# A dense gated layer's first matrix by seven products of quarters in place of eight

## The chip, the cores and the metric

One core of one Trainium2 chip runs the whole program. The metric is device microseconds of one execution. Engines are named as the profile names them: PE (TensorE, with its weight loads as PEld), DVE (VectorE), ACT (ScalarE), POOL (GpSimd) and SP (the queue that issues most transfers).

## The reference, cut to what matters

Two decoder layers for 520 tokens (512 of a prompt and 8 samples), 1024 channels. The change touches the dense gated layer that ends layer 0, and the place of a small compression step of layer 1:

```python
def rmsnorm(x, g):
    x32 = x.astype(F32)
    y = x32 * lax.rsqrt(jnp.mean(x32 * x32, axis=-1, keepdims=True) + EPS) * g.astype(F32)
    return y.astype(x.dtype)

def swiglu(h, w_in, w_out):          # D_FF = 2816
    a, b = jnp.split(h @ w_in, 2, axis=-1)
    return (jax.nn.silu(a) * b) @ w_out
```

Layer 0 is: norm, state-space mixer with a gated output (GELU, then `a * sigmoid(b)`), residual add; norm, `swiglu`, residual add. Layer 1 compresses blocks of the cached rows with a small two-layer network (first matrix 2048 to 128, GELU, second matrix) before its attention.

## The kernel before, in words

Channels lie on the 128 partitions and tokens along a row, so the activations of 1024 channels are a tile of 128 x 8 x 520. Every product is made of f16 parts: an f32 value x is split into a high part xh (ACT copies it to f16) and a low part xl (DVE or POOL subtracts xh from x), and a product is wh·xh + wh·xl + wl·xh, three matmuls that add up in PSUM. `mm3` (from line 230) runs over k (128 input channels each), over the three pairs of parts, and over two column ranges, 256 and 264 tokens. Weights arrive as f32 (`wload`, from line 214): a transfer on the SP queue, an ACT instruction for the high part (line 222), a DVE instruction for the low part (line 223), for 2048 columns at a time; the f32 tile and both f16 tiles have two buffers.

The stages around the change, in order:

- The gated output of the mixer: eight blocks of 2 x 8 x 3 x 2 = 96 matmuls. After each block ACT and DVE empty PSUM (lines 297, 298) and POOL adds to the residual stream `XT` and squares it for the next norm (lines 299, 264, 265).
- `norm` (line 244): two ones-matmuls add up the squares over the partitions (line 249), ACT takes the root, DVE the reciprocal (line 251); then for each of the 8 channel groups k DVE scales (line 254), ACT makes the high part `GH` (line 255), and DVE and POOL in turn make the low part `GL` (line 257).
- `cache_compress`, a generator called with `next`: loads 16 pages of cached rows and splits them (lines 203, 205), loads and splits the first matrix, multiplies the position part (96 matmuls of one column, line 803), and then runs 192 matmuls of 120 columns for the first half of the rows (line 818), before it yields; the second half runs when it is called again after the dense layer. PE has it to do while `norm` is made.
- The dense layer's first matrix: 22 blocks `ob`, each with a transfer of 1 MB, one ACT and one DVE instruction to split it, 96 matmuls, then per column range one ACT Silu (line 324) and one DVE product with the other half (line 325), an ACT copy to f16 `UH` (line 327) and a POOL subtraction to `UL` (line 328).
- The second matrix: 8 blocks over 22 input groups, `XT` updated (line 337), the next norm.

The order of the instructions on each engine's queue is fixed when the program is built, by a planner that gives an earlier line of the source the first turn among what it takes to be ready. On the chip each engine takes its queue strictly in that order. PSUM has 8 banks, handed out in turn by `PS()`.

Of the kernel before, what the change touches and what calls it, by code (L numbers as in the profile page):

```python
# [18 lines left out]
NT = 520  # L19
WS = 256.0  # L20
# [144 lines left out]
def build(tc, a, o, stop=None):  # L165
    nc = tc.nc
    es = ExitStack()
    with es:
# [59 lines left out]
        HV = ((0, 256), (256, NT))  # L228

# [13 lines left out]
        def norm(act, acc, gain):  # L243

            rs = act_pool.tile([128, NT], F32, tag="rs", name=f"rs{cnt[0]}")
            for c0, c1 in HV:
# [4 lines left out]
                V.reciprocal(rs[:, c0:c1], rs[:, c0:c1])  # L251
            for k in range(8):
# [4 lines left out]
                e.tensor_tensor(GL[:, k, :], h, GH[:, k, :], op=ALU.subtract)  # L257

# [30 lines left out]


        for ob in range(8):
            wh, wl = glu_first[ob] if ob < 2 else glu_w(ob)
# [12 lines left out]
        norm(XT, acc, gains[:, 0, :])  # L305
        cs = {}
        cache = cache_compress(tc, nc, a, PS, csp, w1p, wload, hilo, cs)
        next(cache)
        with tc.tile_pool(name="ffn", bufs=1) as fp:

            z = fp.tile([128, 2048], F16, name="z")
# [4 lines left out]
            UH = fp.tile([128, 22, NT], F16, name="UH")  # L316
            UL = fp.tile([128, 22, NT], F16, name="UL")
            for ob in range(22):
                wh, wl = wload(a["w_fin"][:, 2 * ob:2 * ob + 2].rearrange("p b k c -> p (b k c)"), 2048, f"f{ob}")
# [8 lines left out]
                G.tensor_tensor(UL[:, ob, :], sg, UH[:, ob, :], op=ALU.subtract)  # L328
            for ob in range(8):
# [428 lines left out]
def cache_compress(tc, nc, a, PS, cs, w1p, wload, hilo, out):  # L758
# [14 lines left out]
    with tc.tile_pool(name="cc", bufs=1) as cp:  # L773
# [3 lines left out]
        nc.sync.dma_start(wc2, a["w_c2"].rearrange("e s f -> e (s f)"))  # L777
        CS = []
        for b2 in range(4):
            CSH = cp.tile([128, 2, 2, 4, 128], F16, name=f"CSH{b2}")  # L780
            CSL = cp.tile([128, 2, 2, 4, 128], F16, name=f"CSL{b2}")
# [29 lines left out]
        for s in range(2):  # L811
            if s:
                yield
# [1128 lines left out]
```

## Time and profile before

| | us |
|---|---|
| median of 3 runs | 1485.88 (1482.97 to 1486.5) |
| profiled execution, its own time | 1482.78 |
| its span in the trace | 1481.0 |
| first matrix of the dense layer, first to last matmul | 234.0 to 470.2 |

The span is what the trace covers of the profiled execution; its own time is 1.8 us longer for what lies around it. "Busy" of an engine is time in which an instruction of it runs. In a timeline a line is a run of equal instructions: start, the time from the first's start to the last's end, what it is, how many; a bracket gives the idle time ahead of it and what ended that. An instruction that has been issued and is held up inside its engine counts as running.

### The profile page before, as it was taken

Reading aid. Unit: us, or ns where it says so; the run is one execution under the profiler, and the core shown is the slowest. Engines: PE = TensorE matmul, PEld = TensorE weight load, DVE = VectorE, ACT = ScalarE, POOL = GpSimd, SP = SyncE. Lnnn points to the kernel's source line nnn. Section 1 sums busy time; section 2 is a strip of 40 time slices with the busy share of each in tenths; the row PEclk is TensorE's granted clock in tenths of the full one; section 3 lists DMA queues with packets and bytes.
Section 4 is the critical chain, followed back from the end, with each engine's and each line's share of the span. In section 5 each row is a group of like instructions: output and inputs, shape, how many; then the busy total and the mean of one; then the engine's idle time right before and its main releaser. Section 6 shows DMA issues by size and latency. Waiting matters only on the chain. (4 is left out here: it accounts for less than half of the span.)

```text
span 1481.0 us, 37495 instructions
## 1 busy us (share of the span) xinstructions
PE 1355.3 (92%) x15657; PEld 1177.6 (80%) x15657; DVE 943.0 (64%) x1643; ACT 767.4 (52%) x1418; POOL 543.9 (37%) x464
## 2 busy tenths in 40 slices
PE   3869999999999999989989989979997999999994
PEld 2848888888888888766776757848877999999993
DVE  9885565323232323594887886477756888878885
ACT  5526344223232112343887776456645767867772
POOL 4991442222221222211122233306811632724835
PEclk8879999999999999999999999989999999999997
DMA  4124752222322334253313211148999999999984
GB/s 169 61 70 159 263 184 76 96 104 91 110 89 76 120 116 153 93 161 116 100 58 116 82 49 51 46 185 290 357 263 306 369 306 387 361 307 370 325 306 143
DMA packets 82048, 262.34 MB, mean 177 GB/s; under 512 B 25242, under 2 KB 40082, under 8 KB 64338
## 3 DMA queue, kind: packets, MB, share of 16 engines
q1 hardware_dynamic: 78770, 249.24, 49.3%
q0 software_dynamic: 2816, 8.52, 1.7%
q8 instruction: 124, 2.03, 0.6%
q10 hardware_dynamic: 288, 2.14, 0.4%
q14 instruction: 50, 0.41, 0.1%
HBM read 232.30 MB, written 21.67 MB: 171 GB/s over the span
## 5 line engine op out<-in xcount | busy, mean ns | idle before, releaser
L1599 DVE SCALAR_TENSOR_TENSOR ml<-mf,mh 128x2048 f16<-128x2048 f32 (+1 forms) x152 | 310.5, 2046 | 77.1 <-ACT mh L1598 74.3
L1760 PEld LDWEIGHTS <-mh 128*128 128x128 f16 x4224 | 328.9, 98 | 17.9 <-ACT mh L1598 6.5
L1598 ACT ACTIVATE mh<-mf 128x2048 f16<-128x2048 f32 (+1 forms) x152 | 256.0, 1685 | 113.3 <-DMA mf<-in_w_mi 34.9
L1760 PE MATMUL ps<-XE,mh 128*128 128x64 f16 (+7 forms) x2816 | 280.3, 230 | 6.2 <-ACT mh L1598 4.6
L1760 PE MATMUL ps<-XE,ml 128*128 128x96 f16 (+7 forms) x1408 | 262.9, 230 | 2.4 <-DVE ml L1599 2.3
L1840 POOL TENSOR_TENSOR AL<-u,AH 128x272 f16<-128x272 f32 (+3 forms) x88 | 170.0, 1935 | 207.0 <-ACT AH L1839 205.8
L1760 PEld LDWEIGHTS <-ml 128*128 128x128 f16 x2112 | 205.1, 98 | 11.1 <-DVE ml L1599 4.6
L238 PEld LDWEIGHTS <-whf 128*128 128x128 f16 x1408 | 137.7, 98 | 20.2 <-issue 1.7
L238 PE MATMUL ps<-GL,whf 128*128 128x256 f16 x704 | 135.7, 274 | 1.0 <-DVE GL L257 1.0
L238 PE MATMUL ps<-GH,whf 128*128 128x256 f16 x704 | 135.8, 274 | 0.0
L238 PE MATMUL ps<-GH,wlf 128*128 128x256 f16 x704 | 135.6, 274 | 0.0
L1760 PE MATMUL ps<-AH,mh 128*128 128x144 f16 (+7 forms) x704 | 132.1, 229 | 1.5 <-ACT mh L1598 1.5
L1760 PE MATMUL ps<-AL,mh 128*128 128x272 f16 (+7 forms) x704 | 132.6, 229 | 0.9 <-POOL AL L1840 0.9
L1760 PE MATMUL ps<-AH,ml 128*128 128x144 f16 (+7 forms) x704 | 132.1, 229 | 1.3 <-DVE ml L1599 1.3
L328 POOL TENSOR_TENSOR UL<-sf,UH 128x520 f16<-128x520 f32 x22 | 59.4, 2700 | 176.0 <-ACT UH L327 176.0
L325 DVE SCALAR_TENSOR_TENSOR sf<-ps,sf 128x256 f32<-128x256 f32 (+1 forms) x44 | 16.9, 424 | 141.1 <-PE ps L238 141.1
L222 ACT ACTIVATE whf<-wff 128x2048 f16<-128x2048 f32 x22 | 42.0, 1910 | 95.2 <-issue 77.2
L238 PEld LDWEIGHTS <-who 128*128 128x128 f16 x704 | 68.9, 98 | 9.3
L238 PEld LDWEIGHTS <-wlf 128*128 128x128 f16 x704 | 68.9, 98 | 9.2
L1301 ACT ACTIVATE st<-st,mx 128x512 f32<-128x512 f32 (+3 forms) x128 | 71.6, 560 | 6.9 <-DVE mx L1299 6.1
L1299 DVE CUSTOM_DVE_ANT_0 st<-ps,BB 128x512 f32<-128x512 f32 (+3 forms) x128 | 61.2, 485 | 17.7 <-PE ps L1309 15.5
L1309 PE MATMUL ps<-identf,st 128*128 128x128 f32 x320 | 59.9, 288 | 11.8 <-DVE tl L205 7.9
(554 smaller groups left out, 3231.9 us busy)
## 6 DMA issues: line engine op xcount, KB each, us to landing
mf<-in_w_mi SPq DMA_DIRECT2D x88, 1024.0 KB, 7.1
mf<-in_w_mo SPq DMA_DIRECT2D x64, 704.0 KB, 5.8
wff<-in_w_fin SPq DMA_DIRECT2D x22, 1024.0 KB, 4.8
wfo<-in_w_fout SPq DMA_DIRECT2D x16, 704.0 KB, 4.1
wfg<-in_w_glu SPq DMA_DIRECT2D x8, 1024.0 KB, 4.7
wfq<-in_w_qk SPq DMA_DIRECT2D x8, 1024.0 KB, 4.8
HS<-z SPq DMA_DIRECT2D x9, 512.0 KB, 6.0
st<-in_ckc SPq DMA_DIRECT2D x16, 256.0 KB, 3.2
```

Of the source, the lines that this page charges most:

```text
L222: S.activation(wh[:, c], wf[:, c], AF.Copy, scale=WS)
L238: T.matmul(t[:, :c1 - c0], w[:, k0 + k, :], x[k][:, c0:c1] if isinstance(x, list) else x[:, k, c0:c1], start=(first and k == 0 and wi == 0 ...
L325: V.scalar_tensor_tensor(sg[:, c0:c1], tb_[:, :c1 - c0], IWS, sg[:, c0:c1], op0=ALU.mult, op1=ALU.mult)
L328: G.tensor_tensor(UL[:, ob, :], sg, UH[:, ob, :], op=ALU.subtract)
L1299: V.tensor_tensor_reduce(out=st[:, :N], in0=pS[:, :N], in1=bias_cur[0][:, r, 512 - N:], scale=1.0, scalar=3.0e38, op0=ALU.add, op1=ALU.min ...
L1301: S.activation(st[:, :N], st[:, :N], AF.Exp, bias=mx, scale=-1.0, accum_out=st8["sums"][:, 1 + br, r:r + 1])
L1309: T.transpose(pT[:, kb * 128:(kb + 1) * 128], st[:, kb * 128:(kb + 1) * 128], identf)
L1598: S.activation(wh, wf, AF.Copy, scale=WS)
L1599: V.scalar_tensor_tensor(wl, wf, WS, wh, op0=ALU.mult, op1=ALU.subtract)
L1760: T.matmul(ps, w[:, k0 + k, :], x[:, k, :], start=(k == 0 and i == 0), stop=(k == kn - 1 and i == 2))
L1840: al = G.tensor_tensor(AL[r][:, ob], u, AH[r][:, ob], op=ALU.subtract)
```

## The change

The product of the 1024 x 5632 matrix with 1024 x 520 activations is cut into quarters and made by seven products for eight (the Strassen scheme in Winograd's form). Per block `ob`, the weights of a and b and the two halves of the input channels are the four quarters of the weights, each 512 x 128; the two halves of the channels and the two halves of the tokens (260 each) are the four quarters of the activations. `seven` takes the place of `norm`: it makes the four scaled quarters and four sums of them in f32, and splits all seven factors into f16 parts. For each block four sums of weight quarters are made in f32 (three by DVE, one by POOL), and seven factors, 3584 columns for 2048, are split. Each product has 4 x 3 = 12 matmuls of 260 columns. Three PSUM banks hold pairs of products (one holds three); DVE adds between them in five instructions a block. The seventh product of a block and its last steps (`finish`) are put behind the first product of the next block, and a POOL product of the two halves comes new. `cache_compress` is called for its loads, its splits and its position part ahead of block 4 of the mixer's gated output; its first 192 matmuls are called behind that stage and ahead of `seven`. Its split rows become two tiles for one, and the first half's memory is given back before the dense layer.

```diff
+        def seven(act, acc, gain, X, sums):
+            rs = inverse(acc)
+            for k in range(4):
+                h = sums[:, k % 2]
+                for i, q in ((k, h[:, 0:8:7]), (k + 4, h[:, 3:5])):
+                    V.scalar_tensor_tensor(q, act[:, i, :]..., gain[:, i:i + 1], rs..., op0=ALU.mult, op1=ALU.mult)
+                V.tensor_tensor(h[:, 1], h[:, 7], h[:, 0], op=ALU.subtract)
+                G.tensor_tensor(h[:, 5], h[:, 4], h[:, 7], op=ALU.subtract)
+                V.tensor_tensor(h[:, 2], h[:, 4], h[:, 1], op=ALU.subtract)
+                V.tensor_tensor(h[:, 6], h[:, 3], h[:, 2], op=ALU.subtract)
+                for i, c in enumerate((slice(0, 4), slice(4, 7))):
+                    S.copy(X[0][i][:, :, k], h[:, c])
+                    (V, G)[i].tensor_tensor(X[1][i][:, :, k], h[:, c], X[0][i][:, :, k], op=ALU.subtract)
...
         for ob in range(8):
+            if ob == 4:
+                next(cache)
...
-        norm(XT, acc, gains[:, 0, :])
-        cs = {}
-        cache = cache_compress(tc, nc, a, PS, csp, w1p, wload, hilo, cs)
         next(cache)
...
+            sums = fp.tile([128, 2, 8, TH], F32, tag="UL", name="sums")
+            seven(XT, acc, gains[:, 0, :], XS7, sums)
...
-            for ob in range(22):
-                wh, wl = wload(a["w_fin"][:, 2 * ob:2 * ob + 2]..., 2048, f"f{ob}")
-                pa = mm3(wh, wl, 0, 8, GH, GL)
-                pb = mm3(wh, wl, 8, 8, GH, GL)
-                sg = act_pool.tile([128, NT], F32, tag="t2", name=f"sf{ob}", bufs=4)
-                for (c0, c1), ta, tb_ in zip(HV, pa, pb):
-                    S.activation(sg[:, c0:c1], ta[:, :c1 - c0], AF.Silu, scale=IWS)
-                    V.scalar_tensor_tensor(sg[:, c0:c1], tb_[:, :c1 - c0], IWS, sg[:, c0:c1],
-                                           op0=ALU.mult, op1=ALU.mult)
+            def finish(ob, w, b, q, uu, sg):
+                prod(b, w, xs(6), False)
+                V.scalar_tensor_tensor(uu[:, :TH], b[:, :TH], IWS, q[:, :TH], op0=ALU.mult, op1=ALU.add)
+                G.tensor_tensor(sg, sg, uu, op=ALU.mult)
                 S.copy(UH[:, ob, :], sg)
                 G.tensor_tensor(UL[:, ob, :], sg, UH[:, ob, :], op=ALU.subtract)
+            left = None
+            for ob in range(22):
+                wf = wst.tile([128, 4, 512], F32, tag="wf", name=f"wf{ob}")
+                nc.sync.dma_start(wf, a["w_fin"]...)
+                sw = fp.tile([128, 4, 512], F32, tag="sw", name=f"sw{ob}")
+                V.tensor_tensor(sw[:, 0], wf[:, 2], wf[:, 3], op=ALU.add)
+                G.tensor_tensor(sw[:, 2], wf[:, 0], wf[:, 2], op=ALU.subtract)
+                V.tensor_tensor(sw[:, 1], sw[:, 0], wf[:, 0], op=ALU.subtract)
+                V.tensor_tensor(sw[:, 3], wf[:, 1], sw[:, 1], op=ALU.subtract)
+                wa = [wst.tile([128, 4, 512], F16, tag=f"w{x}", name=f"w{x}f{ob}") for x in "hl"]
+                wb = [fp.tile([128, 3, 512], F16, tag=f"w{x}s", name=f"w{x}s{ob}", bufs=2) for x in "hl"]
+                for d, src in ((0, wf[:, 0]), (slice(0, 3), sw[:, 1:4]), (3, sw[:, 0]), (1, wf[:, 1]), (2, wf[:, 3])):
+                    h, l = (wb if src is sw or isinstance(d, slice) else wa)
+                    S.activation(h[:, d], src, AF.Copy, scale=WS)
+                    V.scalar_tensor_tensor(l[:, d], src, WS, h[:, d], op0=ALU.mult, op1=ALU.subtract)
+                prod(pa, wq(wa, 0), xs(0), True)
+                S.activation(q[:, :TH], pa[:, :TH], AF.Copy, scale=IWS)
+                if left is not None:
+                    finish(*left)
+                prod(pb, wq(wb, 0), xs(2), True)
+                V.scalar_tensor_tensor(q[:, TH:], pb[:, :TH], IWS, q[:, :TH], op0=ALU.mult, op1=ALU.add)
+                prod(pc, wq(wa, 3), xs(1), True)
+                V.scalar_tensor_tensor(uu[:, TH:], pc[:, :TH], IWS, q[:, :TH], op0=ALU.mult, op1=ALU.add)
+                prod(pa, wq(wa, 1), xs(3), False)
+                S.activation(sg[:, :TH], pa[:, :TH], AF.Silu, scale=IWS)
+                prod(pb, wq(wb, 1), xs(5), False)
+                V.scalar_tensor_tensor(uu[:, TH:], pb[:, :TH], IWS, uu[:, TH:], op0=ALU.mult, op1=ALU.add)
+                prod(pc, wq(wb, 2), xs(4), False)
+                V.scalar_tensor_tensor(q[:, TH:], pc[:, :TH], IWS, q[:, TH:], op0=ALU.mult, op1=ALU.add)
+                S.activation(sg[:, TH:], q[:, TH:], AF.Silu)
+                left = (ob, wq(wa, 2), pb, q, uu, sg)
+            finish(*left)
```

The tile of zeros `z` moves into the memory of `UH`, and the sums of `seven` into that of `UL`. `sw` has one buffer; the f16 weights have two.

## Rows read from the trace of the kernel before

**Rows 1.** Busy time by stretch: the dense layer's first and second matrix.

```profile
core 0: us, PE busy (x) PEld busy (x) DVE busy (x) ACT busy (x) POOL busy (x), PEclk, DMA share, GB/s
234.00:471.00 237.00, 235.68 (x2125) 207.53 (x2123) 71.19 (x74) 72.75 (x97) 60.52 (x23) 1.00 0.27 90
471.00:588.00 117.00, 117.00 (x1055) 103.32 (x1053) 36.12 (x33) 23.09 (x18) 25.12 (x16) 1.00 0.38 123
```

**Rows 2.** Who waited for whom, 234 to 471 us: total, times, longest.

```profile
DVE sf L325 <- PE ps L238: 141.1, 22, 7.7
...
PE ps L238 <- DVE GL L257: 1.0, 1, 1.0
```

**Rows 3.** The first matrix's matmuls (duration min/median/max, first and last start), weight splits.

```profile
L238 PE MATMUL ps<-GH,whf x704: 272/273/277, 234.0 to 469.8; 128*128 128x256 f16 x176
...
L238 PE MATMUL ps<-GH,wlf x704: 271/274/277, 234.5 to 470.2; 128*128 128x256 f16 x176
L223 DVE SCALAR_TENSOR_TENSOR wlf<-wff,whf x20: 2291/2293/2293, 248.8 to 451.0; 128x2048 f16<-128x2048 f32 x20
...
L223 DVE SCALAR_TENSOR_TENSOR wlo<-wfo,who x16: 1624/1626/2144, 461.1 to 574.1; 128x1408 f16<-128x1408 f32 x16
```

**Rows 4.** DVE, ACT and POOL groups by shape, whole span: busy us, mean ns.

```profile
L1161 DVE TENSOR_TENSOR KL<-kf,KH 64x512 f16<-64x512 f32 x8 | 5.5, 686 | 0.1
L325 DVE SCALAR_TENSOR_TENSOR sf<-ps,sf 128x256 f32<-128x256 f32 x22 | 9.3, 425 | 141.1 <-PE ps L238 141.1
L222 ACT ACTIVATE whq<-wfq 128x512 f16<-128x512 f32 x12 | 6.8, 620 | 1.3 <-PE ps L1098 1.3
L222 ACT ACTIVATE who<-wfo 128x1408 f16<-128x1408 f32 x16 | 22.0, 1377 | 91.6 <-PE ps L238 77.1 <-issue 14.5
L1840 POOL TENSOR_TENSOR AL<-u,AH 128x64 f16<-128x64 f32 x11 | 23.3, 2121 | 0.9
```

**Rows 5.** Timeline of DVE and POOL, 203 to 216 us.

```profile
204.58 1.66 POOL L299 TENSOR_TENSOR XT<-XT,sg 128x520 f32<-128x520 f32 x1 [7.88 <-DVE sg L298]
205.02 3.38 DVE L223 SCALAR_TENSOR_TENSOR wlg<-wfg,whg 128x2048 f16<-128x2048 f32 x1
206.32 2.98 POOL L264 TENSOR_TENSOR q<-XT 128x520 f32<-128x520 f32 x1
...
213.57 1.28 POOL L299 TENSOR_TENSOR XT<-XT,sg 128x520 f32<-128x520 f32 x1 [2.90 <-DVE sg L298]
214.94 1.05 POOL L264 TENSOR_TENSOR q<-XT 128x520 f32<-128x520 f32 x1
```

**Rows 6.** Timeline without PE: one block of the first matrix, 427 to 434 us.

```profile
427.94 0.77 DVE L325 SCALAR_TENSOR_TENSOR sf<-ps,sf 128x256 f32<-128x256 f32 x2 [6.54 <-PE ps L238]
...
429.75 2.29 DVE L223 SCALAR_TENSOR_TENSOR wlf<-wff,whf 128x2048 f16<-128x2048 f32 x1 [1.05 <-ACT whf L222]
430.31 2.76 POOL L328 TENSOR_TENSOR UL<-sf,UH 128x520 f16<-128x520 f32 x1 [7.88 <-ACT UH L327]
```

**Rows 7.** Timeline: DVE instructions with a PSUM operand beside POOL, 104.5 to 108 us.

```profile
105.98 0.65 DVE L642 TENSOR_TENSOR sva<-XS,ps 128x480 f32<-128x480 f32 x1
106.14 0.72 POOL L643 TENSOR_TENSOR sgb<-XS,Ai 128x256 f32<-128x256 f32 x1
```

**Rows 8.** Timeline of DVE in the norm ahead of the first matrix.

```profile
224.18 3.42 DVE L251 RECIPROCAL rs<-rs 128x256 f32<-128x256 f32 x2 [0.49 <-ACT rs L250]
227.72 2.77 DVE L254 SCALAR_TENSOR_TENSOR h<-XT,gains,rs 128x520 f32<-128x520 f32 x4
...
236.36 3.25 DVE L257 TENSOR_TENSOR GL<-h,GH 128x520 f16<-128x520 f32 x2
```

**Rows 9.** The compression's matmuls (lines 803 and 818) and POOL's low parts (line 257).

```profile
L803 PE MATMUL ps<-peh,whc x32: 163/163/168, 219.1 to 222.7; 128*128 128x1 f16 x32
...
L818 PE MATMUL ps<-CSH,whc x128: 218/219/220, 223.3 to 599.8; 128*128 128x120 f16 x128
...
L257 POOL TENSOR_TENSOR GL<-h,GH x4: 1164/1630/2854, 229.9 to 237.4; 128x520 f16<-128x520 f32 x4
```

More of the change, by code (lines that the diff above doesn't have):

```diff
@@ L228, in build @@
         HV = ((0, 256), (256, NT))
+        TH = NT // 2
         def mm3(wh, wl, k0, kn, xh, xl, ps=None, last=True, banks=()):
@@ L241, in mm3, with inverse @@
             return ps
-        def norm(act, acc, gain):
+        def inverse(acc):
             rs = act_pool.tile([128, NT], F32, tag="rs", name=f"rs{cnt[0]}")
@@ L251, in norm @@
                 V.reciprocal(rs[:, c0:c1], rs[:, c0:c1])
+            return rs
+        def norm(act, acc, gain):
+            rs = inverse(acc)
             for k in range(8):
@@ new lines, in build, with xs, prod @@
+            sums = fp.tile([128, 2, 8, TH], F32, tag="UL", name="sums")
+            seven(XT, acc, gains[:, 0, :], XS7, sums)
+            def xs(i):
+                return tuple(x[i // 4][:, i % 4] for x in XS7)
+            def prod(t, w, x, first):
+                for k in range(4):
+                    for i, (ww, xx) in enumerate(((w[0], x[0]), (w[0], x[1]), (w[1], x[0]))):
+                        T.matmul(t[:, :TH], ww[:, k * 128:k * 128 + 128], xx[:, k],
+                                 start=(first and k == 0 and i == 0), stop=(k == 3 and i == 2), skip_group_check=True)
@@ L777, in cache_compress @@
         nc.sync.dma_start(wc2, a["w_c2"].rearrange("e s f -> e (s f)"))
+        c0p = ExitStack()
+        cp0 = c0p.enter_context(tc.tile_pool(name="cc0", bufs=1))
         CS = []
         for b2 in range(4):
-            CSH = cp.tile([128, 2, 2, 4, 128], F16, name=f"CSH{b2}")
-            CSL = cp.tile([128, 2, 2, 4, 128], F16, name=f"CSL{b2}")
-            CS.append((CSH, CSL))
+            CS.append([])
+            for s in range(2):
+                CS[b2].append(tuple((cp0, cp)[s].tile([128, 2, 4, 128], F16, name=f"CS{x}{b2}_{s}") for x in "HL"))
             for bi in range(2):
                 for pg in range(2):
-                    st = cp.tile([128, 512], F32, tag="st", name=f"st{b2}_{bi}_{pg}", bufs=2)
+                    st = cp0.tile([128, 512], F32, tag="st", name=f"st{b2}_{bi}_{pg}", bufs=2)
                     page_dma(st, a["ckc"], 2 * b2 + bi, pg)
-                    hilo(st.rearrange("p (s x a) -> p s x a", s=2, a=8),
-                         *(t[:, :, bi].rearrange("p s k (b a) -> p s (k b) a", a=16)[..., pg * 8:pg * 8 + 8]
-                           for t in (CSH, CSL)))
+                    for s in range(2):
+                        hilo(st.rearrange("p (s x a) -> p s x a", s=2, a=8)[:, s],
+                             *(t[:, bi].rearrange("p k (b a) -> p (k b) a", a=16)[..., pg * 8:pg * 8 + 8]
+                               for t in CS[b2][s]))
         peh = cp.tile([128, 2, 16], F16, name="peh")
@@ L807, in cache_compress @@
             pes.append(pb)
-        hs = cp.tile([128, 480], F32, name="hs")
-        hsh = cp.tile([128, 480], F16, name="hsh")
-        hsl = cp.tile([128, 480], F16, name="hsl")
+        yield
         for s in range(2):
             if s:
+                c0p.close()
                 yield
+            hp = (cp0, cp)[s]
+            hs = hp.tile([128, 480], F32, name="hs")
+            hsh = hp.tile([128, 480], F16, name="hsh")
+            hsl = hp.tile([128, 480], F16, name="hsl")
             pc = PS(6, 7)
```

23 lines of the change are left out of this document (18 added, 5 removed).

## The prediction

> **What bounds the kernel now.** I read the stretches first. Over the dense layer's first matrix PE is busy 235.7 of 237 us at full clock, DVE, ACT and POOL 71, 73 and 61 us [rows 1]: the reader should see an engine that is full beside three that are under a third full. The waits of the same stretch confirm it: DVE waits 141 us for PE, PE 1.0 us for DVE [rows 2]. The stage runs from 234.0 to 470.4 (last start 470.2 and one interval) [rows 3]; that is 2112 matmuls (22 blocks of 96). The second matrix, of the same matmuls (260 columns on average), has 1055 in 117.0 us of a full PE [rows 1]: 110.9 ns each, 10.65 us for 96. So fewer matmuls pay here as long as the three others keep up. The question is whether they do, and that is not read from busy shares.
>
> **DVE and POOL hold each other up.** This I take from timelines. POOL's product XT (520 columns, f32) takes 1.28 us alone, its square q 1.05 us [rows 5]. At 204.58 POOL starts an XT that ends at 206.24; DVE's split wlg, issued at 205.02, takes 3.38 us for the 2.29 us that it has alone [rows 3, 5], and 205.02 + 3.38 - 2.29 = 206.1: it began in earnest when POOL ended. It ends at 208.40; POOL's q, issued at 206.32, ends at 209.30, 0.90 us after that, having taken 2.98. In the stage itself DVE's wlf ends at 432.04, and UL, issued at 430.31, ends 1.03 us later, at 433.07 [rows 6]; a POOL subtraction of 64 columns takes 2.12 us on average where such splits run [rows 4]. So a DVE instruction with two SBUF operands and a POOL product of two tensors run one after the other, whichever came first. One with a PSUM operand is free of this: DVE's 480 columns take 0.65 us with POOL's 256 columns (0.72 us) on top of them [rows 7].
>
> The Trainium skill (GPSIMD Engine Reference, Key points) says that GpSimd shares its SBUF interfaces with VectorE and has contention with instructions in a 2-port mode or with two SBUF inputs. By that rule the same five PSUM instructions of a block stand outside the sum below; the traces agree. Were they inside, with none of their time shared, a block would come to the 11.4 us that stands below as the sum with nothing hidden.
>
> **The change, part by part.** *Matmuls.* A block has 7 x 12 = 84 of 260 columns: 84 x 110.9 ns = 9.32 us for 10.65. With PE as the bound the stage would gain 22 x 1.33 = 29 us.
>
> *DVE in a block.* 512 columns of two SBUF tensors take 0.69 us [rows 4]; from 1408 columns in 1.624 and 2048 in 2.29 us [rows 3] a column costs 1.04 ns, so 1536 take 1.76. Three sums (2.07), four splits of 512 (2.76) and one of 1536 (1.76) are 6.59 us with two SBUF operands. Five instructions from PSUM (0.425 each [rows 4]) are 2.1. Back to back each gains 0.08 (two of 0.425 in 0.77 [rows 6]): 13 instructions, 8.7 - 1.0 = 7.7 us.
>
> *POOL in a block.* One sum of 512 and one product of 520 (1.28 each [rows 5]) and UL (1.16 alone [rows 9]): 3.7 us, or about 3.3 of exclusive time when the start is hidden by waiting, as with UL's 1.03.
>
> *ACT:* 4 x 0.62 + 1.48 (1536 columns, scaled from 512 and 1408 [rows 4]) + the steps on PSUM and UH, under 6 us; not a bound.
>
> *So one block.* Exclusive time of DVE and POOL: 6.59 - 0.6 + 3.4 = 9.4 us, if POOL's other pieces and all of DVE's PSUM work run beside each other. With nothing hidden: 7.7 + 3.7 = 11.4. I also laid the queue out by hand: the last PSUM step, the long split, finish's PSUM step, split, PSUM step, two splits, PSUM step, split, two sums, PSUM step, sum. DVE then waits for POOL's three instructions about 0.8, 0.9 and 1.2 us (two PSUM steps hide 0.35 each), and some 1.2 us for ACT, which can make the 1536 columns' high part only behind the last sum, as `sw` has one buffer: 11.45 us, or 12 with the waits at their longest. The order of this queue is the planner's and no row shows it. A planner that fills the wait for ACT halfway and hides the POOL steps as above gives 7.7 + 3.3 - 0.7 + 0.5 = 10.75. I take this T = 10.75 us, nearer to the hand layout than to the perfect packing because the rows of the stage show POOL and DVE colliding in every block even now, when both are mostly idle; the ends are 9.4 and 12. What was late next would be PE itself: at T over 9.32 it waits for low parts.
>
> The Trainium skill (VectorE: DVE Perf Modes, on the errata of SBUF sources) prices a two-operand VectorE instruction at 58 cycles and one per column, 0.594 us for 512 columns; by it DVE's sum would be 0.7 us less a block and T about 10, the case of no difference below. The row of 0.69 us [rows 4] decides.
>
> *The norm.* Now it takes 11.9 us from the reciprocal's end at 227.7 to 239.6 [rows 8], and PE begins on the first channels at 234.0. `seven` makes per k: two scalings of 520 (0.69 each), three sums of 260 (0.42 each), a low part of 1040 (1.24) on DVE, a difference of 260 (0.72 [rows 7]) and a low part of 780 (1.66, scaled from 1.16) on POOL: 3.9 + 2.4 - 0.6 of overlap = 5.7 us of exclusive time, 22.6 for four. The first product needs all four k, so PE has its result only 1.7 us (POOL's last piece) before the end. What hides it now is the compression (192 matmuls, from 223.3 to 234.0 [rows 3, 9]); it covers ten microseconds, not twenty.
>
> *The compression's position part.* Its matmuls (219.1 to 222.7, with ones-matmuls among them [rows 9]) move into the mixer's gated output, which PE bounds: 3 us later there (0 to 3.7), and gone from behind it. The 16 row loads, their splits (now 32), and two weight loads get an earlier turn on SP, ACT and DVE than blocks 4 to 7 have; I cost that at nothing, as they run within that stage already, and at up to 4 us if PE waits there for a split. The zero fill's transfers wait for `z`, now in memory that the compression frees, and weight transfers may stand behind them on SP; cost nothing, the cover is PE's wait for `seven`, and a few microseconds without it. The second half of the compression stays in place.
>
> **The sum.** Reciprocals end at 227.7 + 3 = 230.7; the first product is made at 230.7 + 22.6 - 1.7 = 251.6; five more products of block 0, and at the very end one, are 6 x 1.33 = 8; 21 blocks follow: the second matrix starts at 259.6 + 21 T, against 470.4. T = 10.75 gives 485.4, **15 us later**. Everything behind is unchanged. The profiled execution is 3.1 us under the median of 1485.9; 1482.8 + 15 = 1497.8 in its terms, 1501 in the median's. The break-even is T = 10.04. About 4.5 us (0.3%) is what a measurement of this kernel can tell from no change.
>
> **Rivals.** *Tight packing.* The planner puts POOL's steps beside DVE's PSUM steps and the wait for ACT vanishes: T = 9.6, the second matrix at 461, 9 us earlier: 1477. For it: 9.4 us is the exclusive sum, and five PSUM steps give cover. Against: both queues are strictly in order. It decides below T = 10.04; between 9.8 and 10.25 nothing is measured.
>
> *The queue waits in full,* as laid out by hand: T = 11.5, 501, 31 us later: 1517. For it: one buffer of `sw` puts sum, high part and low part in one chain.
>
> *PE stays the bound,* the collisions being something else: T = 9.32, and `seven` at DVE's 3.5 us per k (14 us): the first product at 244.7, the second matrix at 448: 22 us earlier, 1464. Rows 5 and 6 speak against it, instruction by instruction.
>
> *The change doesn't do what it says* I leave without a chance of its own: 264 fewer matmuls are written out.
>
> **Chances.** T from 10.25 to 11.1 (forecast): 0.48. In full: 0.22. No measurable difference: 0.11. Tight: 0.13. PE the bound: 0.06. So faster 0.19, same 0.11, slower 0.70. The range goes from T = 9.55 (10 us gained: 1476) to T = 11.6 (33 lost: 1519); outside lie PE as the bound and the tails of the other two. The slower cases alone span 1490 to 1519.
>
> **What would show it.** Right: in the new stage PE well under full, waiting for DVE's low parts; the same event 10.3 to 11 us apart; DVE's sums and splits longer than 0.69 and 1.76 us wherever POOL runs; a hole in PE before the first product of over 10 us. Wrong: blocks 9.3 us apart with PE full, or POOL products of 1.28 us that run beside unslowed splits. If PE waits for anything else (transfers, ACT), the step on T is wrong in its cause.

## The result, and the profile after

The changed kernel takes 1533.81 us (median of 4 runs, 1530.46 to 1536.32) against 1484.91 of the kernel before on the same chip (4 runs, 1482.97 to 1486.5): a ratio of 1.0327, 95% interval 1.0304 to 1.0349. The forecast was 1501, in a range that ended at 1519. Slower was right; 49 us slower, for 15, was not.

The profiled execution has a span of 1534.5 us, 53.5 over the one before. First its busy time over the dense layer's first and second matrix (one row per stretch: engine busy, granted clock), to be held against [rows 1]:

```profile
core 0: us, PE busy (x) PEld busy (x) DVE busy (x) ACT busy (x) POOL busy (x), PEclk, DMA share, GB/s
234.00:523.00 289.00, 229.71 (x1908) 187.02 (x1906) 251.86 (x308) 121.51 (x207) 114.56 (x73) 0.93 0.28 98
523.00:641.00 118.00, 118.00 (x1066) 104.09 (x1065) 36.65 (x33) 23.91 (x19) 25.75 (x16) 1.00 0.37 121
```

The second matrix is what it was (118 us of a full PE, 117 before). The stretch ahead of it grew from 237 to 289 us; PE is busy in 230 of them, DVE in 252 for 71. The bound has changed engines. Where the 53.5 us arise is read from four single rows, the first and last start of an operation: the second matrix's low-part matmuls (line 239), the last PSUM step that belongs to each block (line 400), the copy that follows each block's first product (line 388), and the reciprocals (line 252; the last two belong to a later norm).

```profile
L239 PE MATMUL ps<-UH,wlo x352: 272/274/277, 521.2 to 640.6; 128*128 128x256 f16 x173, 128*128 128x264 f16 x3
...
L400 DVE SCALAR_TENSOR_TENSOR q<-ps,q x22: 410/421/429, 282.0 to 523.1; 128x260 f32<-128x260 f32 x22
...
L388 ACT ACTIVATE q<-ps x22: 366/367/387, 276.5 to 515.4; 128x260 f32<-128x260 f32 x22
...
L252 DVE RECIPROCAL rs<-rs x4: 1745/1748/1753, 239.8 to 646.9; 128x256 f32<-128x256 f32 x2, 128x264 f32<-128x264 f32 x2
```

The last wlo matmul of the second matrix starts at 640.6; before it was 587.3. The difference, 53.3 us, is the whole loss (53.5), so all of it arises ahead of that point. A block's period T is (523.1 - 282.0) / 21 = 11.48 us, forecast 10.75. The first product is copied at 276.5, forecast 251.6. These three readings (last wlo, T, first product) are used for every kernel below, since the totals of single executions also move by up to 12 us from the changed kernel's behind the second matrix, where no edit adds or takes away work.

**The blocks.** The groups by shape from 300 to 520 us (busy us, mean ns of one, idle time before), to be held against 0.69 us for 512 columns in [rows 4]; then two waits of the same stretch (total, times, longest); then DVE's queue and POOL's through one of the longer blocks:

```profile
L378 DVE SCALAR_TENSOR_TENSOR wlf<-wf,whf 128x512 f16<-128x512 f32 x56 | 70.9, 1284 | 0.0
...
L378 DVE SCALAR_TENSOR_TENSOR wls<-sw,whs 128x1536 f16<-128x1536 f32 x18 | 31.7, 1760 | 22.6 <-ACT whs L377 22.6
...
L369 DVE TENSOR_TENSOR sw<-wf 128x512 f32<-128x512 f32 x18 | 21.0, 1165 | 0.0
```

```profile
PE ps L350 <- DVE uu L398: 29.4, 18, 2.4
DVE wls L378 <- ACT whs L377: 22.6, 18, 1.3
```

```profile
386.72 0.42 DVE L400 SCALAR_TENSOR_TENSOR q<-ps,q 128x260 f32<-128x260 f32 x1
388.44 1.76 DVE L378 SCALAR_TENSOR_TENSOR wls<-sw,whs 128x1536 f16<-128x1536 f32 x1 [1.29 <-ACT whs L377]
390.12 0.42 DVE L358 SCALAR_TENSOR_TENSOR uu<-ps,q 128x260 f32<-128x260 f32 x1
390.45 0.42 DVE L392 SCALAR_TENSOR_TENSOR q<-ps,q 128x260 f32<-128x260 f32 x1
390.79 1.73 DVE L378 SCALAR_TENSOR_TENSOR wlf<-wf,whf 128x512 f16<-128x512 f32 x1
392.44 0.68 DVE L378 SCALAR_TENSOR_TENSOR wlf<-sw,whf 128x512 f16<-128x512 f32 x1
393.04 0.41 DVE L394 SCALAR_TENSOR_TENSOR uu<-ps,q 128x260 f32<-128x260 f32 x1
393.38 3.26 DVE L378 SCALAR_TENSOR_TENSOR wlf<-wf,whf 128x512 f16<-128x512 f32 x2
396.56 0.68 DVE L369 TENSOR_TENSOR sw<-wf 128x512 f32<-128x512 f32 x1
397.28 0.69 DVE L371 TENSOR_TENSOR sw<-sw,wf 128x512 f32<-128x512 f32 x1
397.88 0.42 DVE L398 SCALAR_TENSOR_TENSOR uu<-ps,uu 128x260 f32<-128x260 f32 x1
398.22 0.68 DVE L372 TENSOR_TENSOR sw<-wf,sw 128x512 f32<-128x512 f32 x1
398.82 0.42 DVE L400 SCALAR_TENSOR_TENSOR q<-ps,q 128x260 f32<-128x260 f32 x1
```

```profile
390.68 1.29 POOL L359 TENSOR_TENSOR sf<-sf,uu 128x520 f32<-128x520 f32 x1 [6.69 <-ACT whf L377]
393.25 1.26 POOL L370 TENSOR_TENSOR sw<-wf 128x512 f32<-128x512 f32 x1 [1.28 <-issue]
394.48 1.62 POOL L361 TENSOR_TENSOR UL<-sf,UH 128x520 f16<-128x520 f32 x1
```

Put the two queues side by side. The split of 0.68 us takes 1.73 where POOL's product is running, and the next two take 3.26 for 1.28 where POOL has its sum and its low part. The five steps from PSUM keep their 0.42 wherever POOL is. And behind the last sum (line 372, ended at 386.80) DVE waits 1.29 us for ACT's high part of 1536 columns.

DVE is busy 194.7 of these 220 us and waits 22.6 for ACT: its queue has no room left, and sets the pace. PE (183.9 busy) hardly waits for the low parts, for which the prediction's sign had it wait: 29.4 of its 36 idle us are a wait for DVE's step on line 398, which reads a PSUM bank before the seventh product may add to it, and which stands behind splits and sums in DVE's queue. The engine waited for is the one forecast, the instruction is another.

**The start.** ACT's timeline between the gated output's end and the norm, and DVE's reciprocals behind it, against [rows 8]:

```profile
236.64 0.66 ACT L903 ACTIVATE hs<-ps,peb 128x480 f32<-128x480 f32 x1 [6.20 <-PE ps L899]
237.33 0.60 ACT L203 ACTIVATE hsh<-hs 128x480 f16<-128x480 f32 x1
237.96 1.28 ACT L251 ACT_TABLE_LOAD   x1
239.25 0.84 ACT L251 ACTIVATE rs<-ps,epst 128x256 f32<-128x256 f32 x2
```

```profile
239.75 3.42 DVE L252 RECIPROCAL rs<-rs 128x256 f32<-128x256 f32 x2 [1.13 <-ACT rs L251]
```

Line 903 is the compression's GELU, which waits for its 192 matmuls (line 899); only behind it stand the table load and the root of the norm. Before, the norm came first and the compression ran beside it. The reciprocals end at 243.1; forecast 230.7.

So the forecast's error of 38 us (the second matrix began in effect at 523.7, forecast 485.4) falls into three: 12.4 ahead of the reciprocals, 12.5 between them and the first product (33.4 us for 20.9), 13.4 in the blocks.

### The profile page after: what moved, and what is told of

It reads as the page before. It is cut to its first block, busy times and chain, and to the rows that moved or that the text cites. A ratio compares the mean times of both kernels' runs of the same rounds, so it can differ in the third digit from the quotient of the medians.

```text
span 1534.5 us, 37433 instructions
## 1 busy us (share of the span) xinstructions
PE 1348.8 (88%) x15393; PEld 1152.9 (75%) x15393; DVE 1116.6 (73%) x1891; ACT 816.3 (53%) x1544; POOL 595.0 (39%) x512
## 5 line engine op out<-in xcount | busy, mean ns | idle before, releaser
L1841 PE MATMUL ps<-XE,mh 128*128 128x272 f16 (+7 forms) x2816 | 278.8, 229 | 4.4 <-ACT mh L1679 1.8
L1841 PE MATMUL ps<-XE,ml 128*128 128x272 f16 (+7 forms) x1408 | 261.6, 230 | 3.4 <-DVE ml L1680 3.3
L350 PEld LDWEIGHTS <-whf 128*128 128x128 f16 x704 | 70.8, 101 | 47.7 <-issue 35.7
L377 ACT ACTIVATE whs<-sw 128x1536 f16<-128x1536 f32 x22 | 32.6, 1483 | 113.5 <-DVE sw L372 65.5
L350 PE MATMUL ps<-GH,whf 128*128 128x260 f16 x264 | 74.6, 286 | 16.4 <-ACT GH L278 14.9
L378 DVE SCALAR_TENSOR_TENSOR wlf<-wf,whf 128x512 f16<-128x512 f32 x66 | 82.3, 1269 | 0.0
L350 PEld LDWEIGHTS <-whs 128*128 128x128 f16 x528 | 51.8, 99 | 35.4 <-issue 22.2
L350 PE MATMUL ps<-GL,whf 128*128 128x260 f16 x264 | 74.6, 283 | 3.2 <-DVE GL L279 3.2
L350 PE MATMUL ps<-GH,wlf 128*128 128x260 f16 x264 | 74.7, 283 | 1.6 <-DVE wlf L378 1.4
L239 PE MATMUL ps<-UH,who 128*128 128x256 f16 (+1 forms) x352 | 68.9, 275 | 0.0
```

Of the source, the lines that this page charges most:

```text
L239: T.matmul(t[:, :c1 - c0], w[:, k0 + k, :], x[k][:, c0:c1] if isinstance(x, list) else x[:, k, c0:c1], start=(first and k == 0 and wi == 0 ...
L350: T.matmul(t[:, :TH], ww[:, k * 128:k * 128 + 128], xx[:, k], start=(first and k == 0 and i == 0), stop=(k == 3 and i == 2), skip_group_ch ...
L377: S.activation(h[:, d], src, AF.Copy, scale=WS)
L378: V.scalar_tensor_tensor(l[:, d], src, WS, h[:, d], op0=ALU.mult, op1=ALU.subtract)
L1841: T.matmul(ps, w[:, k0 + k, :], x[:, k, :], start=(k == 0 and i == 0), stop=(k == kn - 1 and i == 2))
```

## The experiments

Each is an edit of the changed kernel unless it says otherwise. Numbers 1 to 13 rest on one execution each, the three combined versions at the end on 10 or 12.

**What makes a block 11.48 us?** *1. POOL's three instructions of a block left out.*

```diff
-                G.tensor_tensor(sw[:, 2], wf[:, 0], wf[:, 2], op=ALU.subtract)
-                G.tensor_tensor(sg, sg, uu, op=ALU.mult)
-                G.tensor_tensor(UL[:, ob, :], sg, UH[:, ob, :], op=ALU.subtract)
```

> Leaves out POOL's three instructions of a block: the fourth weight sum, the product of the two halves and the low part of the result (their tiles are filled with zeros once). Theory (DVE and POOL exclude one another): splits and sums fall back to 0.69 and 1.76 us, a block takes 9.3 to 9.9 us, the whole is 33 to 48 us shorter. Rival (DVE's own work and its chain through ACT set the pace): 11 us or more a block, under 12 us gained.

T = 9.18 us, last wlo at 587.8. Every split has its own length again, in the groups by shape from 300 to 470 us:

```profile
L377 DVE SCALAR_TENSOR_TENSOR wlf<-wf,whf 128x512 f16<-128x512 f32 x53 | 35.0, 683 | 0.0
```

DVE is busy 138.8 of 170 us there, 7.5 us a block, and PE all 170. In the changed kernel DVE is busy 152.1 of the same 170 us, 10.3 us a block. So three instructions of an engine that was itself busy 65 of the 170 us lengthen DVE's queue by 2.8 us a block. T falls by 2.3 only, because PE is full now; 9.18 lies a little under the theory's 9.3 to 9.9. (The total, 1480.07 us, is hardly under the 1487.83 of the kernel before beside it, with work left out: the start has already lost what the blocks win.)

*2. POOL's product made twice*, the first into a spare tile.

```diff
+                G.tensor_tensor(act_pool.tile([128, NT], F32, tag="rs", name=f"xt{ob}"), sg, uu, op=ALU.mult)
                 G.tensor_tensor(sg, sg, uu, op=ALU.mult)
```

> POOL makes its product of the two halves twice in each block, the first time into a tile that nobody reads. Theory (exclusive time): DVE is held up by most of another 1.28 us, 12.1 to 12.8 us a block instead of 11.48, the second matrix 13 to 28 us later. Rival (POOL has 7 us a block to spare, and DVE's waits are for PE or ACT): 11.4 to 11.7 us a block, under 5 us later.

T = 12.41 (+0.93), last wlo at 661.7 (+21.1), total 1568.45 us: as the theory has it. Of 1.28 us on POOL 0.93 reach the period.

*3. The same three as copies of one tensor.*

```diff
-                G.tensor_tensor(sw[:, 2], wf[:, 0], wf[:, 2], op=ALU.subtract)
+                G.tensor_copy(sw[:, 2], wf[:, 0])
...
-                G.tensor_tensor(sg, sg, uu, op=ALU.mult)
+                G.tensor_copy(sg, uu)
```

> POOL's three instructions of a block (weight sum, product, low part) become copies of one tensor of the same sizes; what they should compute is left out. If only a POOL instruction that reads two tensors holds DVE's split up: splits near 0.69 and 1.76 us, T 9.2 to 9.9, last start of wlo at 588 to 605. If any POOL instruction on SBUF does: splits of 1.2 and over 2.8 us again, T at least 10.5, last wlo at 618 or later.

T = (485.0 - 279.6) / 21 = 9.78, last wlo at 602.5. In one block of its timelines, with three copies of 0.95 to 1.07 us:

```profile
392.68 0.77 DVE L378 SCALAR_TENSOR_TENSOR wlf<-sw,whf 128x512 f16<-128x512 f32 x1
...
394.31 0.75 DVE L378 SCALAR_TENSOR_TENSOR wlf<-wf,whf 128x512 f16<-128x512 f32 x1
394.99 1.10 DVE L369 TENSOR_TENSOR sw<-wf 128x512 f32<-128x512 f32 x1
```

So mostly the first theory: a copy costs a split or sum beside it 0.1 to 0.4 us, a POOL product of two tensors most of its length (1.05 of 1.29 us above). The splits' mean is 0.87, not the 0.69 expected; DVE is busy 8.5 us a block (147.6 of 170 us), so 1.0 of the 2.8 us stays. These copies are also shorter than the products, so length and number of operands are not fully apart here.

*4. The long split of raw quarters*, so that it waits for no sum.

```diff
-... (slice(0, 3), sw[:, 1:4]), ...
+... (slice(0, 3), wf[:, 0:3]), ...
```

> The long split of a block (1536 columns) is made of the raw quarters instead of the f32 sums; the sums are made as before and three of them not used, so the products are of other weights. Theory (in every block DVE stands 1.3 us until ACT has the high part of the last sum, on top of the exclusive time): 10.1 to 10.6 us a block instead of 11.48, the second matrix 20 to 30 us earlier. Rival (the wait is filled by POOL's turns, which then come elsewhere): 11 us or more a block, under 10 us earlier.

T = 10.34, last wlo at 617.4 (-23.2), and no wait of DVE for ACT is left from 300 to 470 us: the theory's numbers. (The total, 4941.4 us, can't be used: other weights send the tokens of a later routed stage elsewhere, and a long fallback of it runs. Number 8, 4978.51 us, has the same.)

*5. Two buffers for the sums.*

```diff
-                sw = fp.tile([128, 4, 512], F32, tag="sw", name=f"sw{ob}")
+                sw = fp.tile([128, 4, 512], F32, tag="sw", name=f"sw{ob}", bufs=2)
```

> The f32 sums of weight quarters get a second buffer; to make room, the low parts of hidden groups 15 to 21 are written over one another and the second matrix reads others in their place, with the same instructions. Theory (1.3 us of a block are DVE's wait for ACT's high part, which waits for the last sum): the same event of two blocks lies 10.2 to 10.6 us apart instead of 11.5, and the whole is 18 to 28 us shorter. Rival (DVE and POOL excluding one another is all of it, the wait only lets POOL catch up): 11.1 to 11.5 us a block, under 8 us gained.

(To make room, `z` and the factors' sums change places, and the low parts of groups 15 to 21 are written over one another.) T = 11.66, last wlo at 646.9, total 1541.57 us. Inconclusive about the wait: from 300 to 470 us DVE's wait for ACT's long high part falls from 17.4 to 10.1 us, but a wait of 15.9 us for the weights' transfer comes new. In the blocks that still wait for ACT (up to 1.3 us), the planner has put the last sum close ahead of the long high part again: a free buffer does not by itself move an instruction in a queue that is written beforehand.

*6. The long split as three of 512 columns*, the two for the late products at the end, which keeps all the work.

```diff
-... (slice(0, 3), sw[:, 1:4]), (3, sw[:, 0]), (1, wf[:, 1]), (2, wf[:, 3])):
+... (slice(0, 1), sw[:, 1:2]), (3, sw[:, 0]), (1, wf[:, 1]), (2, wf[:, 3]),
+    (slice(2, 3), sw[:, 3:4]), (slice(1, 2), sw[:, 2:3])):
```

> The split of 1536 columns is made as three splits of 512, the two for the late products last. Theory (the wait of 1.3 us for ACT's long high part is part of T, and it comes from one long high part behind the last sum): DVE's wait for it goes, two more instructions cost 0.3 us, T 10.3 to 10.9, last start of wlo 12 to 25 us earlier than 640.6. Rival (the exclusive time of DVE and POOL sets T, the wait only fills a gap that POOL uses): T 11.2 or more, last wlo within 6 us of 640.6.

T = (503.1 - 283.5) / 21 = 10.46, last wlo at 620.6, 20 us sooner, and no wait of DVE for ACT is left from 300 to 470 us: the wait is 1.0 us of T. Smaller pieces in another order remove it; which of the two does it was not separated. The total, 1528.51 us, shows only part of it: its span is 8 us under that of the changed kernel, the other 12 went behind the second matrix in this one execution.

*7. The three POOL instructions made by DVE*, nothing left out.

```diff
-                G.tensor_tensor(sg, sg, uu, op=ALU.mult)
+                V.tensor_tensor(sg, sg, uu, op=ALU.mult)
```

(and so for the sum and the low part.)

> POOL's sum, product and low part of a block are made by DVE, nothing is left out. Theory (exclusive time sets T, and POOL takes 1.28 us for what DVE makes in 0.69): DVE's 7.5 us of a block (138.8 us in 170 at T = 9.18 without POOL's instructions) and 3 x 0.67 come to 9.5; with up to 0.9 of its wait for ACT T is 9.5 to 10.4, last start of wlo at 599 to 618. Rival (DVE is the bound by its own work, and any work moved to it makes the block longer): T over 11.5, last wlo over 640.

T = (478.6 - 281.5) / 21 = 9.39, last wlo at 599.2, total 1504.91 us, 29 under the changed kernel. The full engine gets more work and the block gets 2.1 us shorter. About half of that is the exchange: DVE makes in 0.68 to 0.69 us what POOL needs 1.28 to 1.62 for while it stops DVE for most of that, and DVE's busy time falls from 10.3 to 9.1 us a block (165.6 of 170 us). The other half is the wait for ACT, 1.6 us in all from 300 to 470 us where it was 17.4; why it went with this edit was not tested. The Trainium skill (GPSIMD Engine Reference, Key points) says that for elementwise work DVE is structurally about twice as fast; 0.69 us against 1.28 for 520 columns agrees.

**What makes the first product late?** *8. Blocks 0 and 1 without sums.*

```diff
+                if ob < 2:
+                    sw = wf
+                else:
                     V.tensor_tensor(sw[:, 0], wf[:, 2], wf[:, 3], op=ALU.add)
```

(and so for the other three sums.)

> Blocks 0 and 1 take raw weight quarters for the sums, so that their four sums each are left out and their splits can be made ahead of the norm; all else as in the changed kernel. Theory (the 33 us from the reciprocals to the first product are the seven factors' 23 us and the first two blocks' sums and splits between them): the first product 7 to 11 us sooner behind the reciprocals, the second matrix 6 to 11 us earlier. Rival (the factors' own chain through ACT and POOL takes 30 us): under 3 us.

The first product comes at 270.8, 28.0 us after the reciprocals (242.85) for 33.4: 5.4 us, short of the theory's 7 and over the rival's 3. But the last wlo is at 638.7, only 1.9 sooner: in the end the rival's time, though not by its cause.

*9. The seven factors' step on DVE alone.*

```diff
-                G.tensor_tensor(h[:, 5], h[:, 4], h[:, 7], op=ALU.subtract)
+                V.tensor_tensor(h[:, 5], h[:, 4], h[:, 7], op=ALU.subtract)
...
-                    (V, G)[i].tensor_tensor(X[1][i][:, :, k], h[:, c], X[0][i][:, :, k], op=ALU.subtract)
+                    V.tensor_tensor(X[1][i][:, :, k], h[:, c], X[0][i][:, :, k], op=ALU.subtract)
```

> The changed kernel with the two POOL instructions of the seven factors' step (difference, low part) made by DVE, nothing left out. DVE is busy 36.2 of the 36.5 us from 240 to 276.5, so its queue sets the first product. Theory (POOL's turns stretch that queue: 4 x (0.72 + 1.66) less 4 x 0.6 of overlap, 7.1 us, and DVE makes the same in 4.9): the first product's copy at 271.5 to 274.5 instead of 276.5, the last start of wlo 2 to 5 us sooner than 640.6. Rival (a full DVE only gets more work): copy at 276 or later, last wlo 640 or later.

First product at 272.0, last wlo at 636.1, both 4.5 us sooner: the theory. Total 1528.81 us.

What the 12.5 us over the forecast are is better read from the changed kernel's own trace than from these two gains, which no run shows to add up. Four lines of DVE's timeline; the first three are work of blocks, the fourth is the last two low parts of the factors:

```profile
251.89 1.76 DVE L378 SCALAR_TENSOR_TENSOR wls<-sw,whs 128x1536 f16<-128x1536 f32 x1 [0.25 <-ACT whs L377]
...
254.72 1.76 DVE L369 TENSOR_TENSOR sw<-wf 128x512 f32<-128x512 f32 x1
...
267.63 1.75 DVE L378 SCALAR_TENSOR_TENSOR wls<-sw,whs 128x1536 f16<-128x1536 f32 x1
...
269.63 4.92 DVE L279 TENSOR_TENSOR GL<-sums,GH 128x1040 f16<-128x1040 f32 x2
```

From 243.2 to 274.55, where the last low part ends, DVE is busy 31.1 of 31.4 us: 9.9 in sums and splits of blocks (lines 369 to 378), 0.8 in the compression's `KSL`, the rest, about 21, on the factors themselves. The last 1.9 us to the copy are PE's. So the forecast's 20.9 for the factors was about right, and what was missing is the blocks' work. POOL's turns were in that sum; number 9 gains by taking them away.

*10. The order alone: the kernel before, its eight products kept,* with the compression called as the changed kernel calls it (its loads, splits and position part ahead of block 4, its 192 matmuls ahead of `norm`).

```diff
+            if ob == 4:
+                next(cache)
...
+        next(cache)
         norm(XT, acc, gains[:, 0, :])
...
-        next(cache)
```

> The kernel before with one thing of the change: the compression's loads, splits and position part ahead of block 4 of the gated output, and its first 192 matmuls ahead of the norm; eight products as before. Theory (the norm comes late because of that order): the first matrix starts in earnest 8 to 14 us later than in the kernel before and the whole is 8 to 14 us longer, about 1497. Rival (only the 3 us of the position part are moved): 0 to 4 us longer.

1496.03 us beside 1487.83. The reciprocals end at 241.9 (227.6 in the run beside it), the last wlo starts at 598.6, 11.3 us later: the theory. The order costs this without any change in the products.

*11. The norm's root ahead of the compression.*

```diff
+        rs0 = inverse(acc)
         next(cache)
...
-            rs = inverse(acc)
```

> The norm's sums and root are written ahead of the compression's 192 matmuls again (in the changed kernel they stand behind them on PE, and the root behind the compression's GELU on ACT). Theory (the order put the norm late): the reciprocals end at 233 to 236 us instead of 243.1, and the whole is 7 to 10 us shorter, about 1525. Rival (the splits of the first two blocks' weights fill that time anyway, so the first product is not made earlier): within 3 us of the changed kernel, 1531 to 1537.

The reciprocals end at 235.5, 7.6 us sooner, but the first scaling starts at 242.2. Waits and DVE's timeline from 225 to 245 us say why:

```profile
POOL z L335 <- PE ps L908: 12.8, 1, 12.8
```

```profile
242.23 3.78 DVE L270 SCALAR_TENSOR_TENSOR sums<-XT,gains,rs 128x520 f32<-128x520 f32 x4 [0.66 <-PE ps L908]
```

Line 908 is the last matmul of the compression's first half, which has nothing to do with the norm. What waits for it is memory: `z` and `sums` are tiles of the dense layer's pool, which lies where the compression's first half was. Total 1533.27; the first product comes 3.9 us sooner (272.6), the last wlo 1.0. The theory held for the reciprocals, the rival for the time, by another cause than it gave.

*12. The same with 48 of those 192 matmuls,* to test that reading.

```diff
-                for l in range(16):
+                for l in range(12 * (s == 0), 16):
```

> The run with the norm's sums first, and of the first half's 192 compression matmuls 48 are left in (a quarter of the positions). Theory (the factors cannot begin before the compression ends, since their tiles lie in the dense layer's pool that opens on memory it gives back): the first scaling starts 6 to 8 us earlier than in the run with all 192 (242.2 us there), and so does the second matrix, by 5 to 8 us. Rival (the factors wait for the norm alone, the matmuls are only cover): the scaling starts at the same distance behind the reciprocals (6.8 us), the second matrix within 2 us.

```profile
236.66 2.76 DVE L270 SCALAR_TENSOR_TENSOR sums<-XT,gains,rs 128x520 f32<-128x520 f32 x4
```

The scaling now starts 0.8 us behind the reciprocals (235.9) instead of 6.8, and the last wlo 5.7 us sooner than in number 11. The edit also lets DVE have the compression's split `hsl`, which stood ahead of the scaling in its queue, sooner; but number 11's wait for line 908, of an instruction that reads nothing of it, is there besides. So the memory is what was waited for last. Total 1531.82 us.

*13. Six PSUM banks for the gated output.* That stage ends 7 us later than before (225.7 for 218.7), with a wait of PE of 4.6 us at the position part for DVE's `sg`.

```diff
-            pb = mm3(wh, wl, 8, 8, GH, GL)
+            pb = mm3(wh, wl, 8, 8, GH, GL, banks=B6)
```

(and so for `pa`.)

> The changed kernel with PSUM banks 0 to 5 alone for the mixer's gated output; the compression's position part keeps 6 and 7. Theory (PE's wait of 4.6 us for DVE's sg ahead of the position part is for a bank that a gated block has filled): the wait goes, that stage ends at 221 to 222.5 instead of 225.7, last start of wlo 3 to 5 us sooner. Rival (the wait is for the compression's own weights or comes back elsewhere, as six banks hold one and a half blocks): stage end at 225 or later, last wlo within 1 us of 640.6 or later.

PE's waits at the gated output's matmuls, from 100 to 240 us, now read:

```profile
...
PE ps L239 <- DVE wlg L223: 2.3, 1, 2.3
PE ps L239 <- ACT whg L222: 1.2, 1, 1.2
...
```

The wait for the bank is gone, and the stage ends at 226.6, no sooner: PE waits for the gated output's own weights (1.9 us for `wlg` in the kernel before), and the granted clock is 0.50 at 178 to 180 and at 206 to 208 us. The rival. That the weights are late because the compression's 32 splits stand in the same queues is likely, not shown. (Last wlo at 641.0; of the total, 1545.34, the surplus arises behind it.)

**Do the remedies add up?** *14. Numbers 6, 7 and 11 together.*

> The inverse norm ahead of the compression's 192 matmuls, the long split as three, and POOL's three instructions of a block on DVE, nothing left out. Theory (start and period add up): T 9.4 to 9.9, last start of wlo at 594 to 607, so 1491 to 1504 us: faster than the changed kernel, still slower than the kernel before by 0.3 to 1.4%, because the first product comes some 20 us later than the 29 us of saved matmuls can pay for at T over 9.32. Rival: with POOL out of the way of blocks 0 and 1 too, the first product comes 8 us or more sooner than 276.5 and the total is within 0.3% of the kernel before or under it.

1484.09 us (10 runs), ratio to the kernel before 1.0004, 0.9984 to 1.0023. T = (472.0 - 279.0) / 21 = 9.19, and the stretches show two full engines:

```profile
285.00:470.00 185.00, 184.26 (x1652) 160.18 (x1650) 184.60 (x351) 107.81 (x214) 0.00 (x0) 1.00 0.33 111
```

The total is the rival's, but not by its cause: the first product came 4.9 us sooner (271.6), not 8. The theory's T was too long. PE is the bound again, at 9.19 us for 84 matmuls, and DVE, busy 184.6 of 185, is just as full.

*15. With the seven factors' step on DVE as well* (the edit of number 9).

> The combined kernel (inverse norm early, long split as three, a block's POOL work on DVE), with the seven factors' step on DVE as well. With PE full behind the first blocks (T = 9.19 before this edit), what comes off ahead of the first product comes off the end. Theory: first product's copy at 267 to 270 instead of 271.6, last start of wlo at 586.5 to 590, 1479 to 1482.5 us, a ratio to the kernel before of 0.996 to 0.999. Rival (the DVE work displaced from blocks 0 and 1 comes right behind and is paid there): last wlo 591 or later, no gain.

1481.93 us (12 runs), ratio 0.9998, 0.9981 to 1.0014; first product at 271.4, last wlo at 590.1. The 4.5 us of number 9 do not come again: the rival, nearly. (The total lies in the theory's range, but the kernel before has 1481.96 beside it.) What the two kernels' first matrix looks like is best seen in the last step of each block ahead of its seventh product, here in this kernel:

```profile
L400 DVE SCALAR_TENSOR_TENSOR q<-ps,q x22: 415/418/429, 277.9 to 470.8; 128x260 f32<-128x260 f32 x22
```

and in the step that ends each block of the kernel before:

```profile
L325 DVE SCALAR_TENSOR_TENSOR sf<-ps,sf x44: 422/424/433, 247.1 to 470.8; 128x256 f32<-128x256 f32 x22, 128x264 f32<-128x264 f32 x22
```

One gets there 30.8 us later than the other in its first block, then saves 1.4 us in each of 21, and both are at 470.8 in the last. The seven products then still have the last one to make: the last wlo is 2.8 us later than before. That the totals agree all the same rests on the stages behind, 5.5 us shorter in this execution than in the one before; that this belongs to the edit is not shown.

*16. With six PSUM banks too* (the edit of number 13).

> The same with six PSUM banks for the mixer's gated output. Theory: another 3 to 4 us less, last start of wlo at 583 to 587, 1475 to 1479 us, faster than both kernels. Rival: the compression's loads and splits set the time of its 192 matmuls and of the seven factors' memory, so the stage end moves and the first product does not: as the kernel without the edit.

1485.53 us (12 runs), ratio 1.0021, 1.0005 to 1.0037; first product at 271.8, last wlo at 590.4. The rival: nothing comes of it, and if anything it is slower. No version here that keeps all the work beats the kernel before.

## Why the prediction was right or wrong, step by step

- **DVE and POOL run one after the other, steps from PSUM are free of it: right.** Experiments 1 and 2 show it from both sides (2.8 us of DVE's queue a block less without POOL's three, 0.93 more with a fourth), and the block's timeline instruction by instruction. DVE's own work was forecast at 7.7 us a block and measured 7.5; POOL's share, 3.3 less 0.7, measured 2.8. The case by which sums would be cheaper and T about 10 is decided against: sums that nothing holds up take 0.67 to 0.69 us here, as in [rows 4]. The Trainium skill (VectorE: DVE Perf Modes, on the errata of SBUF sources) itself says below its table that the row the prediction used is too low, and gives 0.691 us for an f32 add of 512 columns; the trace agrees.
- **T = 10.75 from a planner that halves the wait for ACT and hides POOL's steps: wrong, 11.48.** The queue laid out by hand was nearly the order on the chip, and the rival "the queue waits in full" (11.5) was the right one. Its 11.45 is in part luck: the terms written beside it (7.7, 0.8, 0.9, 1.2 and 1.2) add up to 11.8. Measured, a block is 7.5 of DVE's own, 2.8 of POOL and 1.2 of the wait for ACT. I took the middle for no better reason than that the order was not known, and so put the wait at 0.5. It stands in nearly every block; taking it away gives 10.46 and 10.34 (experiments 6 and 4), under the forecast. The cause was in the text, and more than half of it was taken off without a row. 21 times 0.73 are 15.3 us; the 8 us forecast for block 0 and the last product were 6.1, which leaves 13.4.
- **Reciprocals at 230.7, "3 us later": wrong, 243.1.** This is the step that failed outright. I counted the position part's 3 us, and of the moved 192 matmuls only that they no longer hide the factors' step. That they now stand ahead of the norm on PE, and that GELU and a table load of 1.28 us stand ahead of the root on ACT, was in the diff (`next(cache)` ahead of `seven`) and not in the sum. Experiment 10: 11.3 us at the end from the order alone. Experiment 11: 7.6 of the reciprocals' 12.4 us from that one call; the other 4.8 are mostly the next point's. And even with the order repaired the memory given back by the compression holds the first scaling (experiments 11 and 12), which I had seen for `z` only and costed at nothing.
- **Position part into the gated output, 0 to 4 us if PE waits for a split: the bound was about right, the value was not.** The stage ends 7 us later: some 3 for the matmuls, 4.6 for a wait and some more for a granted clock of 0.50 behind it (180 to 184 us), less the 1.9 that the kernel before waited for a split. I had taken nothing. Experiment 13 shows that this is not the PSUM bank's doing alone: with the bank free, other waits and the clock take as much.
- **The first product 20.9 us behind the reciprocals: wrong, 33.4.** The sum was of the factors' step alone, and for that it was about right (some 21 us of DVE's queue). DVE was busy 36.2 of the 36.5 us to 276.5, with 9.9 us of sums and splits of blocks in between, which the planner put into the same queue; I costed that work only inside its own blocks. Leaving the first two blocks' sums out gives back 5.4 us (experiment 8).
- **Break-even and what is late next: right in kind.** At PE's bound a block takes 9.19 us (forecast 9.32), and experiment 15 shows both queues repaired and the time unchanged: the start costs what the blocks save. That the start could weigh as much as the blocks was not among my rivals; all but one varied T alone, and that one only shortened the start. With the first product at 276.5 and the 8 us for block 0, the forecast's own sum puts the break-even at T = (470.4 - 276.5 - 8) / 21 = 8.85, and at 9.09 with the 271.6 of experiment 14. Both lie under the 9.19 at which PE is full, so with this start no repair of the blocks alone could win.

## What to carry to other kernels

Fewer matmuls move the bound to the engine that makes their operands: count that engine's queue in order, with every wait for the largest piece another engine must make first, and take the order as it comes out unless a row shows better. Elementwise work of two tensors given to POOL was not free here beside DVE instructions with two SBUF operands; where DVE makes it twice as fast, giving it back to DVE can shorten a block even when DVE is the bound. When a call is moved, list all that it issues on each engine ahead of the critical chain, its table loads and the memory that it holds included: a saving that starts 30 us late is gone.

## What was not expected of the hardware

Between the reciprocals and the first product PE gets its matmuls in trickles, and the granted clock falls to 0.50, the lower of its two levels (1.2 GHz). The changed kernel's stretches, with the columns of the first fence:

```profile
240.00:250.00 10.00, 0.00 (x0) 0.00 (x0) 9.94 (x14) 1.33 (x4) 6.29 (x4) 0.65 0.82 325
250.00:260.00 10.00, 5.23 (x23) 3.08 (x23) 9.75 (x10) 5.51 (x6) 6.28 (x3) 0.50 0.77 273
260.00:270.00 10.00, 4.52 (x19) 2.13 (x18) 10.00 (x15) 4.43 (x5) 3.47 (x4) 0.50 0.31 106
```

It fell after PE had run full to the end of the compression's matmuls and then stood idle from 240 to 250 us; from 276.5 to 290, with PE full, it is 0.98 again. The loss was not measured by itself. DVE is full in the same rows, so up to 272 us PE waited for operands; from there to 276.5 it runs without a gap, its matmuls starting 0.22 us apart for 0.11 at full clock, so at most some 2 us are the clock's (an estimate from these starts).

And a POOL copy of one tensor costs a DVE split or sum beside it 0.1 to 0.4 us (experiment 3), where a POOL product of two tensors costs a split 1.05 (1.73 for 0.68 in the block shown). I had expected all or nothing.
